# A one-layer encoder on one core: lo parts of weights on VectorE alone, a shorter first pass of the output projection, and a fixed order for the forms of the second norm

## The chip, the cores and the metric

The kernel runs on one core of a Trainium2 chip. A core has TensorE (PE in the views; its weight loads are listed apart as PEld), VectorE (DVE), ScalarE (ACT), GpSimd (POOL) and SyncE (SP), which here starts nearly all the transfers (DMAs) from the chip's memory (HBM). Each engine works through its own queue of instructions in order, and the engines wait for one another by semaphores. The on-chip memory that all of them read is SBUF; PSUM is the small memory into which TensorE writes its sums. The metric is the time of one execution on the device in microseconds (us), and the number to predict is the median of such runs.

## The reference: what is computed

One layer of an encoder over 512 tokens of 1024 channels, in float32. The part before the change's place is told in words here: an RMS norm, one input projection to 7680 columns, a pooling mixer, a differential attention, a two-way gated recurrence, and three sigmoid gates. What the change touches is from the last up-projection to the end:

```python
    gates = jax.nn.sigmoid(gate_pre.reshape(B, S, N_BRANCHES, D_MODEL))
    merged = (gates[:, :, 0] * (y_pool @ w_up_pool[l])
              + gates[:, :, 1] * (y_attn @ w_up_attn[l])
              + gates[:, :, 2] * (y_rec @ w_up_rec[l]))
    x = x + merged @ w_out[l]

    h2 = rms_norm(x, norm2_g[l])
    gu = h2 @ w_ffn_in[l]
    x = x + (jax.nn.silu(gu[..., :FFN_HIDDEN]) * gu[..., FFN_HIDDEN:]) @ w_ffn_out[l]
return rms_norm(x, final_norm_g)
```

The hidden width `FFN_HIDDEN` is 2816.

## The kernel before

**Split numbers.** Every large product is made of three products in a shorter float format (`fp32r`): each operand is split into a hi part, the number rounded to that format, and a lo part, what is left; then hi by hi, lo by hi and hi by lo are added in PSUM. For a weight, `split_w` (L179 to L184) does it: ScalarE copies the raw weight to `whi` (L182) and another engine subtracts `whi` from the raw weight to give `wlo` (L183). Which engine does the subtraction is taken from a cycle, `lo_engine`. It is VectorE alone at first; from the attention's branch through the output projection and the second norm GpSimd and VectorE take turns, beginning with GpSimd; in the first FFN product it is VectorE alone; in the second FFN product the two take turns again.

**Loading and splitting ahead.** `Jobs` holds the list of products in order. A chunk of weights of 1 MB, loaded by SyncE (L161) into one of two raw buffers, holds two parts, and a part is split into one of three pairs of buffers (`wsp`) while earlier products still run. A raw buffer is free for the next load when the lo parts of its chunk are written. The last half of the output projection has a pool of its own for its four parts (`LAST["wp"]`, four pairs), so these parts don't wait for `wsp`.

**Order.** The matmuls keep the order in which the code gives them. On the other engines the framework that builds the program places instructions by a planner of its own (`schedule_with_timeline_sim=True`), which takes what is ready by its own costs, earlier code first. So the order on ScalarE and VectorE is read from the trace and can differ from that of the code; `tc.issue_after(i)` forces an instruction to stand behind `i` when both are on the same engine.

**The up-projection's end.** The last eight products of the attention branch give `merged`, one row tile of 128 channels each: VectorE multiplies the sum by the gate (L582) and adds it to `merged` (L583), ScalarE writes `m_hi` (L586), VectorE writes `m_lo` (L587). These are the k-tiles 0 to 7 of the output projection.

**The output projection.** `w_out` has 1024 columns. Columns 0 to 255 (called Q0 here) and 256 to 511 (Q1) are jobs of `out_quarter_job`, of two parts each: part a holds k-tiles 0 to 3, part b k-tiles 4 to 7. Columns 512 to 1023 are one job, `out_last_job`, of four parts with two k-tiles each (L0 to L3 here). Q0 and Q1 take four blocks of 128 tokens, 8 k-tiles and three terms, so 96 matmuls of 256 columns each. When Q0 starts, the last `m_hi` and `m_lo` aren't there yet; so its first three blocks leave the last k-tile out at first (21 matmuls each), in three open sums, and take it up afterwards. Each block's sum is added to the residual by VectorE (L999, L1008).

**The second norm.** For each of the four blocks: mean square on ScalarE (L405), `rstd` on GpSimd, scaling on VectorE (L411), transposes on TensorE, hi (L424) and lo (L426) of the transposed rows, and a full copy (L428).

**Forms.** The first FFN product multiplies 2 by 2 blocks of weights and rows with seven products in place of eight, so it needs four combinations of row blocks, the forms `n1`, `n2`, `d` and `n4`. `Forms.make` (L324 to L348) has VectorE make the combinations `v` (L341 to L345), ScalarE their hi parts `fhi` (L336) and VectorE their lo parts `flo` (L338). The code's order of the lo parts is `n1`, `n2`, `d`, `n4`. The weights' side needs sums of weights (L260 to L264) with parts `shi` and `slo`.

**The first FFN product.** `ffn_start_job` begins it: two products of the first pair that need no form, and the whole of column tile 0, gate and up, in plain form, whose SiLU and product are `ffn_pair_evac(0)` (L1039, L1040). Then the first pair goes on with `n1` and `n2` (`second`), `d` (`third`) and `n4` (`fourth`). ScalarE copies sums to `u` (L1109) and `g` (L1112); VectorE adds to `g` (L1118) before `n4` may be written to the same bank. The weights of pairs 2 and 3 are split only behind `FF["forms"].last` (`PairPart.split`, L278), which before is the lo part of `n2` on VectorE alone.

**The second FFN product** has 11 steps for each half of the columns, of 24 matmuls of 512 columns; the hidden rows are split by ScalarE (L1056) and VectorE (L1057), and one weight part is split for each step.

Of the kernel before, what the change touches and what calls it, by code (L numbers as in the profile page):

```python
# [11 lines left out]
F32 = mybir.dt.float32  # L12
# [3 lines left out]
ALU = mybir.AluOpType  # L16
PSUM = bass.MemoryType.PSUM

P = 128
# [57 lines left out]
def encoder_kernel(ctx: ExitStack, tc: tile.TileContext, x, norm1_g, w_in, pool_w, pool_scale,  # L77
# [98 lines left out]

    lo_engine = [cycle([nc.vector])]

    def split_w(view, a, b, wpool=None):  # L179
        hi = (wpool or wsp).tile([P, a, b], F32R, name="whi")  # L180
        lo = (wpool or wsp).tile([P, a, b], F32R, name="wlo")
        nc.scalar.copy(out=hi, in_=view)  # L182
        next(lo_engine[0]).tensor_tensor(out=lo, in0=view, in1=hi.bitcast(F32), op=ALU.subtract)  # L183
        return hi, lo  # L184
# [56 lines left out]
    class PairChunk:  # L241
# [14 lines left out]
        def add(self):  # L256
# [7 lines left out]
            nc.vector.tensor_tensor(out=sums[:, 1], in0=sums[:, 3], in1=w12, op=ALU.add)  # L264

    class PairPart:

# [47 lines left out]
    class Forms:  # L315
# [8 lines left out]
        def make(self, pool_, full, v):  # L324
# [8 lines left out]
            order = ("d", "n2", "n1", "n4")  # L333

            def done(i):
                nc.scalar.copy(out=hi[:, i], in_=v[i])  # L336
                setattr(self, order[i], (hi[:, i], lo[:, i]))
                return nc.vector.tensor_tensor(out=lo[:, i], in0=v[i], in1=hi[:, i].bitcast(F32), op=ALU.subtract).ins  # L338

            stt = nc.vector.scalar_tensor_tensor  # L340
# [645 lines left out]
    def out_quarter_job(cs, first):  # L986
        def body(*parts):
            m, x2 = LAST["m"], LAST["x2"]
            pss = {}

            for b in range(3 if first else 0):
                pss[b] = bank("mm")[:, 0:256]
                yield from rows_mm(pss[b], m, slice(b * P, (b + 1) * P), parts, 4, range(KT - 1))
            for b in range(NB):
                ps = pss.get(b)
                if ps is None:
                    ps = bank("mm")[:, 0:256]
                yield from rows_mm(ps, m, slice(b * P, (b + 1) * P), parts, 4, range(KT - 1 if b in pss else 0, KT))
                nc.vector.tensor_tensor(out=x2[:, b, cs], in0=x2[:, b, cs], in1=ps, op=ALU.add)  # L999
        return body  # L1000
# [241 lines left out]

    lo_engine[0] = cycle([nc.gpsimd, nc.vector])
    stM = ExitStack()
# [27 lines left out]
    with ExitStack() as st:  # L1272
        sums = hp2.tile([P, KT, S], F32, name="hid2")
        FF["forms"].make(st.enter_context(pool("forms")), full, sums)
        FF["hid"] = [p.tile([P, 8, S], F32, name=n) for p, n in ((hp2, "hid2"), (hp, "hid"), (hp2, "hid2"))]
        ffn_pair_evac(0, *FF["first"])
        jobs.limit = 4
        lo_engine[0] = cycle([nc.vector])
        pipe.run([jobs.stream(n_ffn - n_out)])
    lo_engine[0] = cycle([nc.gpsimd, nc.vector])  # L1280
    FF["g"] = ctx.enter_context(pool("gf")).tile([P, D], F32, name="gfb")
# [53 lines left out]
```

## Time and profile before

| what | value |
|---|---|
| median of 3 runs | 926.35 us |
| the runs | 932.74, 924.45, 926.35 us |
| the profiled execution | 932.13 us |
| its span, first to last instruction | 930.3 us |
| mean granted TensorE clock | 0.994 |
| TensorE, VectorE, ScalarE, GpSimd busy | 898.0, 578.2, 419.6, 113.0 us |
| lo parts of weights on GpSimd | 19, mean 2399 ns |
| lo parts of weights on VectorE | 127, mean 1168 ns |

Rows of the timeline begin with the start and the duration in us, then the engine, the line, the operation, the tile written and those read, the shapes and the count; in square brackets stands how long the engine was idle before and which instruction ended that. SPq is SyncE's queue. In the rows of windows the busy times of the five engines are followed by the granted TensorE clock (1.00 is full), the share of the DMA engines that was busy, and GB/s. In the view of waits each row gives the total in us, the count and the longest.

### The profile page before, as it was taken

What the parts mean: (1) busy time and instruction counts of PE and PEld (TensorE: products, weight loads), DVE (VectorE), ACT (ScalarE), POOL (GpSimd) and SP (SyncE); (2) the same over time, 40 slices, a digit from 0 to 9 for tenths busy, and PEclk for the clock granted to TensorE, in tenths of its full rate; (3) what the DMA queues carried; (4) which work ended last, traced back from release to release, by engine and by line L of the source; (5) the groups of instructions that cost most, each with busy time, mean ns of one, the idle gap of its engine ahead of it and who ended that gap; (6) DMA issues with size and microseconds to landing.
All of it is one profiled execution on the core that took longest, in us unless ns stands there. A gap on an engine that the chain in (4) does not pass through costs nothing.

```text
span 930.3 us, 13178 instructions
## 1 busy us (share of the span) xinstructions
PE 898.0 (97%) x5341; PEld 790.8 (85%) x5341; DVE 578.2 (62%) x849; ACT 419.6 (45%) x652; POOL 113.0 (12%) x93
## 2 busy tenths in 40 slices
PE   5998999999999999999999989899999999999996
PEld 4887987888898888788888888899999999988885
DVE  5686553754858864634423635998888888635644
ACT  5544423533646673332233324655555555533433
POOL 2143311310000000000022231000000000022222
PEclk9999999999999999999999989999999999999999
DMA  8322031314034115422222450143433433422312
GB/s 248 89 75 68 3 90 34 103 46 153 25 110 132 48 46 170 157 91 91 91 91 91 132 163 1 46 136 94 133 93 99 127 93 104 136 78 91 94 65 91
DMA packets 106313, 89.00 MB, mean 96 GB/s; under 512 B 2687, under 2 KB 93325, under 8 KB 106125
## 3 DMA queue, kind: packets, MB, share of 16 engines
q1 hardware_dynamic: 105532, 86.59, 30.4%
q10 hardware_dynamic: 720, 1.57, 0.4%
q8 instruction: 42, 0.69, 0.3%
q14 instruction: 19, 0.15, 0.0%
HBM read 86.06 MB, written 2.10 MB: 95 GB/s over the span
## 4 chain that ended last, share of the span: by engine, by line
PE 82%; DVE 5%; ACT 1%; issue 1%; POOL 1%; DMA 1%; POOLq 0%; ACTq 0%; DVEq 0%
PE mm L90 56%; PE rc L90 21%; PE tp L90 4%; PE tp L98 1%; DVE wlo L183 1%; DMA raw<-in_w_out_dram 1%; POOL wlo L183 1%; DVE kq L731 1%; ACT whi L182 0%; DVE flo L338 0%; DVE pyr L741 0%; DVE slo L290 0%; DVE sums L260 0%; DVE l L824 0%; DVE pt L746 0%
## 5 line engine op out<-in xcount | busy, mean ns | idle before, releaser
L182 ACT CAST whi<-raw 128x1024 fp32r<-128x1024 f32 (+1 forms) x146 | 143.9, 990 | 208.5 <-PE mm L90 120.3
L183 DVE TENSOR_TENSOR wlo<-raw,whi 128x1024 fp32r<-128x1024 f32 x127 | 148.1, 1168 | 140.4 <-PE mm L90 80.3
L90 PE MATMUL mm<-hT_hi,whi 128*128 128x512 f32 (+1 forms) x440 | 110.0, 387 | 0.4 <-ACT hT_hi L424 0.4
L90 PE MATMUL mm<-hT_hi,wlo 128*128 128x512 f32 (+1 forms) x440 | 108.4, 383 | 0.0
L90 PE MATMUL mm<-hT_lo,whi 128*128 128x512 f32 (+1 forms) x440 | 107.5, 382 | 0.4 <-DVE hT_lo L426 0.4
L183 POOL TENSOR_TENSOR wlo<-raw,whi 128x1024 fp32r<-128x1024 f32 x19 | 45.6, 2399 | 470.1 <-ACT whi L182 351.3
L90 PEld LDWEIGHTS mm<-hT_lo,whi 128*128 128x128 f32 x440 | 79.1, 188 | 15.6 <-DVE hT_lo L426 0.6
L90 PEld LDWEIGHTS mm<-hT_hi,whi 128*128 128x128 f32 x440 | 78.4, 188 | 16.4 <-issue 1.9
L90 PEld LDWEIGHTS mm<-hT_hi,wlo 128*128 128x128 f32 x440 | 78.8, 188 | 15.4 <-issue 1.0
L290 DVE TENSOR_TENSOR slo<-sums,shi 128x1024 fp32r<-128x1024 f32 x42 | 51.4, 1223 | 17.3 <-ACT shi L288 17.3
L288 ACT CAST shi<-sums 128x1024 fp32r<-128x1024 f32 x42 | 44.1, 1050 | 39.9 <-issue 25.6
L1057 DVE TENSOR_TENSOR hlo<-hid,hhi 128x1024 fp32r<-128x1024 f32 x20 | 34.9, 1753 | 25.8 <-ACT hhi L1056 25.8
L734 POOL TENSOR_TENSOR kq<-kq,pyr 128x512 f32<-128x512 f32 x24 | 34.3, 1428 | 45.4 <-ACT kc L700 27.2
L90 PEld LDWEIGHTS rc<-kq,kc 128*128 128x128 f32 x224 | 29.7, 191 | 6.6 <-issue 2.7
L90 PE MATMUL rc<-kq,kc 128*128 128x128 f32 x224 | 32.1, 287 | 2.9 <-DVE kq L731 2.9
L731 DVE TENSOR_TENSOR kq<-kq,pyr 128x256 f32<-128x256 f32 x56 | 26.2, 507 | 14.0 <-PE rc L90 13.9
L700 ACT COPY kc<-kq 128x512 f32<-128x512 f32 x28 | 18.7, 668 | 32.0 <-POOL kq L734 22.8
L858 ACT ACTIVATE s<-s,mx 128x512 f32<-128x512 f32 x32 | 23.0, 720 | 16.1 <-DVE mx L856 16.0
L90 PE MATMUL mm<-flo,shi 128*128 128x256 f32 x168 | 26.7, 281 | 0.9 <-DVE flo L338 0.9
L90 PE MATMUL mm<-fhi,shi 128*128 128x256 f32 x168 | 26.7, 281 | 0.5 <-ACT u L1109 0.5
L90 PE MATMUL mm<-fhi,slo 128*128 128x256 f32 x168 | 26.6, 281 | 0.0
L90 PE MATMUL mm<-y_hi,whi 128*128 128x512 f32 x96 | 26.4, 393 | 0.0
(255 smaller groups left out, 1858.5 us busy)
## 6 DMA issues: line engine op xcount, KB each, us to landing
raw<-in_w_ffn_in_dram SPq DMA_DIRECT2D x44, 512.0 KB, 5.3
raw<-in_w_in_dram SPq DMA_DIRECT2D x18, 1024.0 KB, 5.2
raw<-in_w_in_dram SPq DMA_DIRECT2D x24, 512.0 KB, 4.2
raw<-in_w_ffn_out_dram SPq DMA_DIRECT2D x10, 1024.0 KB, 5.1
raw<-in_w_out_dram SPq DMA_DIRECT2D x4, 1024.0 KB, 5.3
xin<-in_x_dram SPq DMA_DIRECT2D x4, 512.0 KB, 9.0
raw<-in_w_up_rec_dram SPq DMA_DIRECT2D x2, 1024.0 KB, 7.7
x<-in_x_dram SPq DMA_DIRECT2D x1, 2048.0 KB
```

What stands on the lines that cost most here:

```text
L90: i = nc.tensor.matmul(out_, lhsT=lhsT, rhs=rhs, start=start, stop=stop, skip_group_check=chain)
L98: tc.keep_in_program_order(nc.tensor.transpose(out_, in_, idn))
L182: nc.scalar.copy(out=hi, in_=view)
L183: next(lo_engine[0]).tensor_tensor(out=lo, in0=view, in1=hi.bitcast(F32), op=ALU.subtract)
L288: nc.scalar.copy(out=hi, in_=view)
L290: nc.vector.tensor_tensor(out=lo, in0=view, in1=hi.bitcast(F32), op=ALU.subtract)
L700: nc.scalar.copy(out=strided(kc, 0, [[2 * n, S // (2 * n)], [n, 2], [1, n]]), in_=strided(kq, 2 * S, [[2 * n, S // (2 * n)], [S + n, 2], [ ...
L731: nc.vector.tensor_tensor(out=xv, in0=xv, in1=tv, op=ALU.mult)
L734: (nc.gpsimd if n < 128 else nc.vector).tensor_tensor(out=xv, in0=xv, in1=tv, op=ALU.mult)
L858: nc.scalar.activation(out=s, in_=s, func=AF.Exp, scale=-1.0, bias=mx[:, c:c + 1], accum_out=zz[:, i, c:c + 1])
L1057: nc.vector.tensor_tensor(out=lo, in0=view, in1=hi.bitcast(F32), op=ALU.subtract)
```

## The change

It does three things.

First, `lo_engine` is gone and `split_w` always uses VectorE; the 19 subtractions that GpSimd did are VectorE's.

Second, the first three blocks of Q0 leave out the last two k-tiles at first, not the last one: 18 matmuls each, and then six for each in place of three. The number of matmuls is the same.

Third, in `Forms.make` every VectorE instruction is placed behind the one before it, so the order on VectorE is that of the code. `done` returns both its ScalarE and its VectorE instruction. The splits for pairs 2 and 3 now stand behind both of `n2` (before: the VectorE one), and the SiLU and the product of column tile 0 stand behind both of `n4`, on ScalarE and on VectorE; before nothing held them. `issue_after` puts an order on one engine and no wait between engines.

```diff
     def split_w(view, a, b, wpool=None):
...
-        next(lo_engine[0]).tensor_tensor(out=lo, in0=view, in1=hi.bitcast(F32), op=ALU.subtract)
+        nc.vector.tensor_tensor(out=lo, in0=view, in1=hi.bitcast(F32), op=ALU.subtract)
...
+    @contextmanager
+    def behind(after):
+        with ExitStack() as st:
+            for i in after:
+                st.enter_context(tc.issue_after(i))
+            yield
...
         def split(self):
-            with tc.issue_after(FF["forms"].last) if self.chunk.behind else ExitStack():
+            with behind(FF["forms"].last) if self.chunk.behind else ExitStack():
                 self.sums_and_split()
...
+            last = [None]
+            def dve(form, **kw):
+                with tc.issue_after(last[0]) if last[0] else ExitStack():
+                    last[0] = form(**kw).ins
             def done(i):
-                nc.scalar.copy(out=hi[:, i], in_=v[i])
+                on_act = nc.scalar.copy(out=hi[:, i], in_=v[i]).ins
                 setattr(self, order[i], (hi[:, i], lo[:, i]))
-                return nc.vector.tensor_tensor(out=lo[:, i], in0=v[i], in1=hi[:, i].bitcast(F32), op=ALU.subtract).ins
+                dve(tt, out=lo[:, i], in0=v[i], in1=hi[:, i].bitcast(F32), op=ALU.subtract)
+                return on_act, last[0]
...
-            nc.vector.tensor_tensor(out=v[2], in0=f["r11"], in1=f["r12"], op=ALU.subtract)
-            nc.vector.tensor_tensor(out=v[0], in0=f["r22"], in1=f["r12"], op=ALU.subtract)
-            stt(out=v[1], in0=v[0], scalar=-1.0, in1=f["r11"], op0=ALU.mult, op1=ALU.subtract)
+            dve(tt, out=v[2], in0=f["r11"], in1=f["r12"], op=ALU.subtract)
+            dve(tt, out=v[0], in0=f["r22"], in1=f["r12"], op=ALU.subtract)
+            dve(stt, out=v[1], in0=v[0], scalar=-1.0, in1=f["r11"], op0=ALU.mult, op1=ALU.subtract)
             done(2)
-            stt(out=v[3], in0=v[1], scalar=-1.0, in1=f["r21"], op0=ALU.mult, op1=ALU.subtract)
+            dve(stt, out=v[3], in0=v[1], scalar=-1.0, in1=f["r21"], op0=ALU.mult, op1=ALU.subtract)
             self.last = done(1)
             done(0)
-            done(3)
+            self.end = done(3)
...
             for b in range(3 if first else 0):
                 pss[b] = bank("mm")[:, 0:256]
-                yield from rows_mm(pss[b], m, slice(b * P, (b + 1) * P), parts, 4, range(KT - 1))
+                yield from rows_mm(pss[b], m, slice(b * P, (b + 1) * P), parts, 4, range(KT - 2))
...
-                yield from rows_mm(ps, m, slice(b * P, (b + 1) * P), parts, 4, range(KT - 1 if b in pss else 0, KT))
+                yield from rows_mm(ps, m, slice(b * P, (b + 1) * P), parts, 4, range(KT - 2 if b in pss else 0, KT))
...
-        ffn_pair_evac(0, *FF["first"])
+        with behind(FF["forms"].end):
+            ffn_pair_evac(0, *FF["first"])
```

More of the change, by code (lines that the diff above doesn't have):

```diff
@@ L1 @@
-from contextlib import ExitStack
-from itertools import cycle, islice
+from contextlib import ExitStack, contextmanager
+from itertools import islice
 import numpy as np
@@ L175, in split @@
             self.chunk.left -= 1
-    lo_engine = [cycle([nc.vector])]
     def split_w(view, a, b, wpool=None):
@@ L1241, in encoder_kernel @@
         pipe.run([pool_mix(), jobs.stream(n_pool - n_att)])
-    lo_engine[0] = cycle([nc.gpsimd, nc.vector])
     stM = ExitStack()
@@ L1275, in encoder_kernel @@
         FF["hid"] = [p.tile([P, 8, S], F32, name=n) for p, n in ((hp2, "hid2"), (hp, "hid"), (hp2, "hid2"))]
-        ffn_pair_evac(0, *FF["first"])
+        with behind(FF["forms"].end):
+            ffn_pair_evac(0, *FF["first"])
         jobs.limit = 4
-        lo_engine[0] = cycle([nc.vector])
         pipe.run([jobs.stream(n_ffn - n_out)])
-    lo_engine[0] = cycle([nc.gpsimd, nc.vector])
     FF["g"] = ctx.enter_context(pool("gf")).tile([P, D], F32, name="gfb")
```

2 lines of the change are left out of this document (1 added, 1 removed).

## The prediction

> **What bounds the kernel now.** I read the page's first lines, then TensorE's waits, then the timeline around each wait that the change can touch.
>
> ```profile
> span 930.3 us, 13178 instructions
> PE 898.0 (97%) x5341; PEld 790.8 (85%) x5341; DVE 578.2 (62%) x849; ACT 419.6 (45%) x652; POOL 113.0 (12%) x93
> ```
> ```profile
> PE tp L98 <- DVE hT_lo L426: 2.1, 1, 2.1
> PE mm L90 <- ACT whi L182: 1.9, 1, 1.9
> PE mm L90 <- POOL wlo L183: 1.0, 1, 1.0
> PE mm L90 <- DVE flo L338: 0.9, 1, 0.9
> PE mm L90 <- DVE g L1118: 0.9, 1, 0.9
> PE mm L90 <- ACT m_hi L586: 0.6, 1, 0.6
> PE mm L90 <- DVE m_lo L587: 0.6, 1, 0.6
> ```
>
> TensorE is busy for 97% of the span: it is the bound, and only what keeps it waiting can be won. Of the seven waits (total, count, longest) the last six are in reach of this change, 5.9 us together; the first lies near the start and is needed for the clock below. A wait costs more than its row where the clock falls after it, so the output projection (Q0 and Q1) has to be seen in time, by rows of its timeline (many between them are left out) and of its windows:
>
> ```profile
> 517.44 0.69 DVE L583 TENSOR_TENSOR merged<-merged,gate 128x512 f32<-128x512 f32 x1
> 519.82 2.40 POOL L183 TENSOR_TENSOR wlo<-raw,whi 128x1024 fp32r<-128x1024 f32 x1 [8.78 <-ACT whi L182]
> 520.16 2.60 DVE L583 TENSOR_TENSOR merged<-merged,gate 128x512 f32<-128x512 f32 x1
> 524.67 0.87 PE L90 MATMUL mm<-whi,m_hi 128*128 128x256 f32 x6
> 528.53 1.23 DVE L183 TENSOR_TENSOR wlo<-raw,whi 128x1024 fp32r<-128x1024 f32 x1
> 528.79 0.87 PEld L90 LDWEIGHTS mm<-whi,m_hi 128*128 128x128 f32 x7
> 529.35 0.61 ACT L586 CAST m_hi<-merged 128x512 fp32r<-128x512 f32 x1
> 529.52 2.48 POOL L183 TENSOR_TENSOR wlo<-raw,whi 128x1024 fp32r<-128x1024 f32 x1 [7.30 <-ACT whi L182]
> 529.58 0.87 PEld L90 LDWEIGHTS mm<-whi,m_lo 128*128 128x128 f32 x7
> 530.00 2.56 DVE L587 TENSOR_TENSOR m_lo<-merged,m_hi 128x512 fp32r<-128x512 f32 x1 [0.24 <-ACT m_hi L586]
> 532.03 0.37 SPq L161 DMA_DIRECT2D raw<-in_w_out_dram  x1
> 534.20 1.10 DVE L999 TENSOR_TENSOR x<-x,mm 128x256 f32<-128x256 f32 x3 [1.64 <-PE mm L90]
> 537.15 2.94 ACT L182 CAST whi<-raw 128x1024 fp32r<-128x1024 f32 x3 [7.18 <-DMA raw<-in_w_out_dram]
> 537.60 0.63 PE L90 MATMUL mm<-whi,m_hi 128*128 128x256 f32 x4
> 539.22 4.78 POOL L183 TENSOR_TENSOR wlo<-raw,whi 128x1024 fp32r<-128x1024 f32 x2 [7.21 <-ACT whi L182]
> 540.14 0.73 PE L90 MATMUL mm<-whi,m_hi 128*128 128x256 f32 x4 [1.90 <-ACT whi L182]
> 544.05 1.22 PE L90 MATMUL mm<-wlo,m_hi 128*128 128x256 f32 x4 [1.02 <-POOL wlo L183]
> 554.64 0.63 PE L90 MATMUL mm<-whi,m_hi 128*128 128x512 f32 x2
> ```
> ```profile
> 20.00:30.00 10.00, 7.88 (x63) 7.34 (x63) 5.73 (x17) 2.29 (x5) 0.00 (x0) 1.00 0.38 104
> 541.00:542.00 1.00, 1.00 (x8) 1.00 (x8) 0.00 (x0) 0.00 (x0) 1.00 (x2) 0.59 0.00 0
> 548.00:549.00 1.00, 1.00 (x11) 1.00 (x10) 0.15 (x1) 0.00 (x0) 0.00 (x0) 0.99 1.17 292
> ```
>
> Seven matmuls of 256 columns take 529.58 - 528.79 = 0.79 us, so one takes 0.113 and the 96 of Q0 or of Q1 10.85. Q0 runs from 524.67 to 537.60, 2.08 too long: the two waits for k-tile 6 (0.6 and 0.6) and the refilling of TensorE's pipeline after them. Q1 runs from 537.60 to 554.64, 17.04, or 6.19 too long. Of that 1.90 is the wait for the hi part of its part b, 1.02 that for its lo part; the other 3.27 is mostly the clock, which the last two rows (clock: the third figure from the right) show at half from about 541.2 to 548.0, 6.8 us. So 8.27 us stand here against an unhindered TensorE.
>
> Why Q1b comes late can be read too. GpSimd ends L1's lo part at 532.00, which frees a raw buffer; the load of L2 and L3 is issued at 532.03; ScalarE starts at 537.15, on its landing, three hi parts in a row, ending at 540.09; TensorE goes on at 540.14. So the third of the three is Q1b's, and it stands behind L2's and L3's on ScalarE, though the code has it first.
>
> **Part 1: lo parts on VectorE.** Removed: 19 GpSimd subtractions (2.40 each here). Added: 19 on VectorE, 1.23 each. In most places that costs nothing, since TensorE doesn't wait:
>
> ```profile
> 470.00:480.00 10.00, 10.00 (x45) 8.27 (x45) 1.23 (x1) 2.67 (x4) 2.39 (x1) 1.00 0.24 80
> 860.00:870.00 10.00, 10.00 (x46) 8.27 (x45) 8.17 (x11) 5.86 (x10) 1.53 (x2) 1.00 0.32 105
> ```
>
> In the attention's branch VectorE has 8.8 of 10 us free. In the second FFN product the fullest stretch is 860 to 870: 8.17 plus one part, 9.4 of 10. The cover is that parts are split some steps ahead; were it gone there, one late part would cost up to 1.2 us, once. I take 0.
>
> In the output projection it counts. VectorE's subtractions beside GpSimd's are stretched: L583 took 2.60 at 520.16 against 0.69 at 517.44, and L587 2.56. Both end just after GpSimd's. So VectorE gets back 1.9 + 1.9 and takes over two parts of 1.23 there: 1.3 us less load, not more. The Trainium skill, "Perfetto Trace Analysis", section "Optimizing Scalar/DVE Operations", speaks against this move: with VectorE saturated, work offloaded to another engine, GpSimd even, may pay, though it adds that the two share a port, so it might not help. By the first half of that rule 2.5 us of load are added here with none handed back, L1's lo part below ends about 1.9 later and as much of the gain below is gone; the stretched rows side with the second half.
>
> L1's lo part would then follow L0's (ends 529.76). With the last m_lo first (0.7) it ends at 531.9. Before it, and all of VectorE 0.7 earlier (the 1.9 of L583 back, less the 1.23 of Q0b's lo part, which GpSimd did at 519.82), at 530.3. I take 531.1, 0.9 us before GpSimd's end; ends 530.3 and 531.9.
>
> **Part 2: two k-tiles left out.** No instruction more or less. The first pass has 54 matmuls, 6.1 us, and ends at 530.8 without touching k-tiles 6 and 7; the last m_hi ends at 529.96 and the last m_lo, unstretched, at about 530.7 (or 531.9 behind L1's lo part). So both waits go, and Q0 ends at 524.67 + 10.85 = 535.5, 2.1 earlier.
>
> Nearly all of that is eaten at once, for Q1's part b is next, and it hangs on the load, not on TensorE. Load issued at 531.1, the same 5.1 us to ScalarE's start: 536.2. If Q1b's hi part stays third, TensorE goes on at 539.2, second at 538.2; I take 538.8. Q1 has stopped at 535.5 + 0.45 = 536.0, so the wait *grows* from 1.9 to 2.8, but ends 1.3 sooner. Q1b's lo part on VectorE, last of three, ends at 540.9 (537.2 + 3 x 1.23), and TensorE wants it 16 matmuls, 1.8 us, after going on, at 540.6: 0 to 0.3, so about 1 of the 1.02 is gone. The remaining 92 matmuls end at 549.2, plus the clock.
>
> For the clock: 1.9 and 1.02 close together were followed by half speed; the 2.1 us gap in the 20 to 30 row by none (1.00). A single 2.8 us gap may do either; it costs between 0 and the 3.27 above; I take the middle, 1.5. Q1 ends at 550.7: **3.9 us gained** of 8.27. The Trainium skill, "TensorE: Matmul & The Clock Gate", section "Part 1: The HAM clock gate", says that activity is judged in free-running windows of about 3.4 us; the 6.8 us above is two of them, and by that rule a gap with no second wait behind it costs one window, 1.7 us, or nothing, by its phase, which no run need share with another; with 1.7 the gain is 3.7, with 0 it is 5.4.
>
> **Part 3: the forms.**
>
> ```profile
> 589.01 1.28 ACT L1039 ACT_TABLE_LOAD   x1
> 590.80 1.04 ACT L182 CAST whi<-raw 128x1024 fp32r<-128x1024 f32 x1
> 591.75 2.94 ACT L336 CAST fhi<-hid 128x1024 fp32r<-128x1024 f32 x3
> 592.83 1.23 DVE L338 TENSOR_TENSOR flo<-hid,fhi 128x1024 fp32r<-128x1024 f32 x1 [0.92 <-ACT fhi L336]
> 595.10 2.35 DVE L338 TENSOR_TENSOR flo<-hid,fhi 128x1024 fp32r<-128x1024 f32 x2
> 597.51 0.73 PE L90 MATMUL mm<-flo,shi 128*128 128x256 f32 x4 [0.92 <-DVE flo L338]
> 598.73 0.37 ACT L1109 COPY u<-mm 128x256 f32<-128x256 f32 x1 [2.19 <-PE mm L90]
> 600.84 1.22 DVE L338 TENSOR_TENSOR flo<-hid,fhi 128x1024 fp32r<-128x1024 f32 x1
> ```
>
> Before the first `fhi` ScalarE does a table load, the SiLU (together 1.8, 589.01 to 590.80) and a weight part of pair 2 (1.04). VectorE idles 0.92 for the first `fhi`; and TensorE, which wanted the lo part of `n2` at 596.59 (597.51 less 0.92), gets it at the end of the pair that began at 595.10, 597.45: `n2` is the second of that pair, behind `d`. After: the three go behind the forms, so the 0.92 of VectorE goes, and `n2` comes before `d`, another 1.2 earlier. So `n2` is ready at 597.45 - 0.92 - 1.2 = 595.3, and TensorE's 0.92 goes.
>
> The added order holds table load and SiLU until `n4`'s hi part is done: its combination ends before `n2`'s lo part begins, 594.1, plus 1.0 for the hi part and 1.8 is 596.9. Behind them on ScalarE queue the copies to `g` and `u`, and TensorE waits for `u`, now at 598.73, then at 597.8. So 0.9 covers it; if a weight part of pair 2 (1.04) comes between, up to 0.6 is lost. The product L1040 is behind `n4`'s lo part on VectorE, and nothing of TensorE's waits for it here. Late next is the 0.9 for `g` (L1118): VectorE is packed to there, but `n4`'s 1.22 at 600.84 has moved up; so that wait becomes anything from 0 to 0.9, and I take 0.6. Sum: 0.9 + 0.3 = **1.2** gained, ends 0.3 and 1.8.
>
> **The sum** against the profiled execution: 3.9 + 1.2 = 5.1; its time is 930.3 of span and 1.8 around it, 932.1, so 927.0. The median of the runs, 926.35, lies 5.8 below that execution. If its run didn't have the half clock, 2.9 (6.8 less 1.0 of waiting, halved) of my gain isn't there to be had: 2.2, so 924.2; if it had, 921.3. I take the middle, 922.7.
>
> **The rivals.**
>
> *A: the wait for Q1b goes altogether.* ScalarE takes Q1b's hi part first, as soon as Q0 leaves its buffer at about 534.2, before the load of L2 lands. For it: the code's order; Q0 is 2.1 earlier and the load only 0.9. Against it: in the trace the planner put it behind both. Then all of 8.3 goes, with 1.2 for the forms 9.5; by the two readings of the median 916.9 or 919.8, so 918.3.
>
> *B: slower, by VectorE's queue.* L1's lo part lands behind the three L999 additions (534.20 now), which wait for the second pass: the third block's sum is done at 530.8 + 18 x 0.113 = 532.8, its addition by 533.4, then 1.23: 534.6. Load 5.1, three copies 2.94: TensorE goes on at 542.7 after idling 6.7 us; 10.4 and the 3.3 of the clock follow, so Q1 ends at 556.4, 1.8 late. Less 1.2 for the forms it is 0.6 slower than a baseline with the half clock and 3.5 slower than one without: 926.9 or 929.9, so 928.4. It decides from an end of L1's lo part of about 534.1. For it: the planner has put late code ahead of early code here. Against: that part's inputs are ready some 3 us before the last addition's.
>
> *C: part 2 does nothing.* If m_lo of k-tile 6 was never late without the stretched rows, all is part 1's; then the time is that of the forecast, and only the credit differs.
>
> **How the numbers follow.** Forecast (wait shortened at its end but not gone, C included): 0.65; A 0.20; B 0.12; 0.03 for what I don't see. The range takes in A's and B's times: 917 to 929, wide because the three runs span 924.45 to 932.74. One per cent, 9.3 us, is about what a measurement of this kernel can tell from no change. Faster by over 1% is A in its better half and little else: 0.14; slower by over 1%: 0.05; within: 0.81.
>
> **What would show it.** Right: no GpSimd `wlo`; L583 and L587 all near 0.69; no wait for m_hi or m_lo in Q0; the load of L2 issued by 532; a wait for `whi` at Q1's start of 2 to 3 us ending before 539.5; none for `wlo`; none for `flo`. Wrong: that wait absent (A), or past 542 (B), or TensorE waits after 800.

## The result, and the profile after

| what | before | after |
|---|---|---|
| median of 7 runs | 932.74 us | 919.20 us |
| the runs | 924.45 to 933.57 us | 917.68 to 926.52 us |
| the profiled execution | 932.13 us | 917.68 us |
| mean granted TensorE clock in it | 0.994 | 0.997 |

The ratio after to before is 0.990, with a 95% interval of 0.985 to 0.9945. The forecast was 922.7 us with a range of 917 to 929, so the time lies in it, 3.5 us under the likeliest value.

One thing has to be said before any of these numbers is read. The runs of either kernel lie in two groups about 8 us apart, and which group a run falls into goes with a pace of TensorE that is shown further down. Over all the comparisons made here the kernel before was run 71 times: 49 times between 922.75 and 928.58 (middle 925.5) and 22 times between 931.57 and 935.06 (middle 933.6). Of the seven runs in the table four are of the upper group. Of the seven after, six lie between 917.68 and 922.33 (middle 919.0) and one is 926.52. Lower group against lower group, the change is worth 925.5 - 919.0 = 6.5 us; the 13.5 us between the two medians of the table is that and the luck of the groups. The ratio of 0.990 holds some of this luck too: lower group against lower group it is 0.993.

The first two lines of the page after:

```profile
span 915.9 us, 13166 instructions
PE 887.4 (97%) x5341; PEld 781.0 (85%) x5341; DVE 583.4 (64%) x868; ACT 418.9 (46%) x652; POOL 66.8 (7%) x74
```

GpSimd has its 19 subtractions less (93 to 74 instructions, 113.0 to 66.8 us), VectorE 19 more (849 to 868) for only 5.2 us more of busy time, since its own instructions are no longer stretched beside GpSimd's (the additions to `merged`, the `m_lo` and the lo parts of the hidden rows take 16.4 us less together).

To see where the 14.4 us between the two profiled spans (930.3 and 915.9) went, I cut both traces at the first matmul of each stage:

| stage, us | before | after | won |
|---|---|---|---|
| start to Q0 | 524.67 | 524.74 | -0.07 |
| Q0 | 12.93 | 11.31 | 1.62 |
| Q1 | 17.04 | 12.65 | 4.39 |
| L0 to the first matmul of `n4` (second norm and forms lie in it) | 48.41 | 47.40 | 1.01 |
| `n4` to the second FFN product (pairs 1 to 21) | 199.38 | 191.88 | 7.50 |
| second FFN product | 119.45 | 119.47 | -0.02 |

The change's own stages give 1.62 + 4.39 + 1.01 = 7.0 us. The largest row, 7.50, lies where the change does nothing. First the stages it does touch. Rows of the timeline after, in the output projection (the line numbers are those of the kernel after: `whi` L180, `wlo` L181, `merged` L597, `m_lo` L601):

```profile
521.25 0.68 DVE L597 TENSOR_TENSOR merged<-merged,gate 128x512 f32<-128x512 f32 x1
524.74 0.87 PE L90 MATMUL mm<-whi,m_hi 128*128 128x256 f32 x6
527.61 2.36 DVE L181 TENSOR_TENSOR wlo<-raw,whi 128x1024 fp32r<-128x1024 f32 x2 [0.23 <-ACT whi L180]
529.88 0.69 DVE L601 TENSOR_TENSOR m_lo<-merged,m_hi 128x512 fp32r<-128x512 f32 x1
529.99 0.37 SPq L161 DMA_DIRECT2D raw<-in_w_out_dram  x1
535.01 2.94 ACT L180 CAST whi<-raw 128x1024 fp32r<-128x1024 f32 x3 [5.96 <-DMA raw<-in_w_out_dram]
536.05 0.63 PE L90 MATMUL mm<-whi,m_hi 128*128 128x256 f32 x4
538.00 0.74 PE L90 MATMUL mm<-whi,m_hi 128*128 128x256 f32 x4 [1.32 <-ACT whi L180]
548.71 1.54 PE L90 MATMUL mm<-whi,m_hi 128*128 128x512 f32 x6
```
```profile
536.00:543.00 7.00, 5.68 (x48) 5.42 (x48) 4.25 (x5) 2.07 (x4) 0.00 (x0) 1.00 0.42 121
543.00:549.00 6.00, 6.00 (x54) 5.96 (x54) 2.30 (x4) 2.34 (x3) 0.00 (x0) 1.00 1.15 290
```

No stretched L597 or L601 is left (2.60 and 2.56 before). L0's and L1's lo parts run as a pair from 527.61 and end at 529.97, ahead of the last `m_lo`; the load goes out at 529.99 (532.03 before); ScalarE begins 5.0 us later and does three hi parts, and TensorE goes on at 538.00, when the third is done. So Q1b is still the third of the three. Q0 runs without a wait, and the one wait left in Q1 is 1.32 us, with the clock at full speed throughout (the third figure from the right, 1.00 in both rows).

The forms: the addition to `g` in the timeline before, then the timeline after (combinations and `flo` are L346, `fhi` L349, the product of column tile 0 L1054, the addition to `g` L1132):

```profile
602.58 0.42 DVE L1118 TENSOR_TENSOR g<-mm,g 128x256 f32<-128x256 f32 x1
```
```profile
588.16 2.35 DVE L346 TENSOR_TENSOR flo<-hid,fhi 128x1024 fp32r<-128x1024 f32 x2
590.43 1.22 DVE L258 TENSOR_TENSOR sums<-raw 128x1024 f32<-128x1024 f32 x1
591.56 1.82 DVE L181 TENSOR_TENSOR wlo<-raw,whi 128x1024 fp32r<-128x1024 f32 x2
592.02 0.74 PE L90 MATMUL mm<-fhi,shi 128*128 128x256 f32 x4 [0.46 <-ACT u L1123]
593.30 1.22 DVE L346 TENSOR_TENSOR flo<-hid,fhi 128x1024 fp32r<-128x1024 f32 x1
594.44 0.68 DVE L1054 TENSOR_TENSOR hid<-rc,silu 128x512 f32<-128x512 f32 x1
595.04 0.68 DVE L261 TENSOR_TENSOR sums<-sums,raw 128x512 f32<-128x512 f32 x1
595.64 0.41 DVE L1132 TENSOR_TENSOR g<-mm,g 128x256 f32<-128x256 f32 x1
596.11 0.74 PE L90 MATMUL mm<-fhi,whi 128*128 128x256 f32 x4 [1.08 <-DVE g L1132]
```

The lo parts of `n2` and `d` are a pair from 588.16, `n2` first now, and TensorE no longer waits for one. But the wait for `g` is 1.08, not smaller than the 0.89 of before. From the start of that pair to the addition to `g` VectorE does eight instructions without a pause: the lo parts of `n2`, `d` and `n4`, two sums and two lo parts of pair 2, and the product of column tile 0. In before it is the same eight in another order, and both times they take 7.48 us (595.10 to 602.58 before, 588.16 to 595.64 after). The fixed order moves the lo part of `n4` among them; it takes none of them out. What the change moves is their start, from 40.46 us after the first matmul of L0 to 39.45, because VectorE's idle 0.92 before its first `flo` is gone. The addition to `g`, and `n4` behind it, come earlier by that 1.0 and no more.

Now the 7.50 us. The same two windows in both traces, before first; the first two busy times, with their counts, are TensorE's matmuls and its weight loads:

```profile
700.00:710.00 10.00, 10.00 (x88) 10.00 (x87) 8.21 (x10) 5.50 (x11) 0.00 (x0) 1.00 0.39 107
750.00:760.00 10.00, 10.00 (x87) 10.00 (x86) 8.32 (x11) 5.39 (x9) 0.00 (x0) 1.00 0.39 107
```
```profile
700.00:710.00 10.00, 10.00 (x90) 10.00 (x90) 8.71 (x12) 5.34 (x9) 0.00 (x0) 1.00 0.42 118
750.00:760.00 10.00, 10.00 (x91) 10.00 (x89) 8.71 (x11) 5.82 (x10) 0.00 (x0) 1.00 0.42 113
```

TensorE is full, the clock is granted whole, nothing waits, and yet before does 87 to 88 matmuls in 10 us and after 90 to 91. By their starts the matmuls of 256 columns come every 0.118 us before and every 0.113 after, to the end of that product. The stretch holds the 12 matmuls of pair 1's `n4` and 84 for each of 20 pairs, 1692: 199.38 / 1692 = 0.1178 and 191.88 / 1692 = 0.1134, and that is the 7.5 us. In before the products ahead of it ran at 0.113 to 0.114, and 0.118 began with the matmul that ended the wait for `g`. In after it was 0.118 in Q0 and 0.113 after the wait for `whi` that ended at 538.00.

### The profile page after: what moved, and what is told of

Read it like the earlier page. It is cut to its first block, busy times and chain, and to the rows that moved or that the text cites. A ratio compares the mean times of both kernels' runs of the same rounds, so it can differ in the third digit from the quotient of the medians.

```text
span 915.9 us, 13166 instructions
## 1 busy us (share of the span) xinstructions
PE 887.4 (97%) x5341; PEld 781.0 (85%) x5341; DVE 583.4 (64%) x868; ACT 418.9 (46%) x652; POOL 66.8 (7%) x74
## 4 chain that ended last, share of the span: by engine, by line
PE 83%; DVE 6%; DMA 1%; ACT 1%; issue 1%; POOL 1%; POOLq 0%; ACTq 0%; DVEq 0%
PE mm L90 56%; PE rc L90 21%; PE tp L90 4%; DVE wlo L181 2%; PE tp L98 1%; DMA raw<-in_w_out_dram 1%; DVE kq L745 1%; DVE hid L346 0%; DVE flo L346 0%; POOL kq L748 0%; ACT whi L180 0%; DVE pyr L755 0%; DVE sums L258 0%; DVE slo L296 0%; DVE l L838 0%
## 5 line engine op out<-in xcount | busy, mean ns | idle before, releaser
L181 DVE TENSOR_TENSOR wlo<-raw,whi 128x1024 fp32r<-128x1024 f32 (+1 forms) x146 | 170.2, 1169 | 168.5 <-PE mm L90 85.0
L180 ACT CAST whi<-raw 128x1024 fp32r<-128x1024 f32 (+1 forms) x146 | 143.8, 990 | 202.6 <-PE mm L90 116.8
L90 PEld LDWEIGHTS mm<-hT_hi,whi 128*128 128x128 f32 x440 | 78.4, 188 | 16.4 <-issue 1.9
L90 PE MATMUL mm<-y_lo,whi 128*128 128x512 f32 x96 | 26.2, 392 | 0.0
L258 DVE TENSOR_TENSOR sums<-raw 128x1024 f32<-128x1024 f32 x21 | 25.7, 1224 | 0.6
L90 PE MATMUL mm<-y_hi,wlo 128*128 128x512 f32 x96 | 25.9, 390 | 0.0
L90 PE MATMUL mm<-flo,shi 128*128 128x256 f32 x168 | 25.9, 276 | 0.0
```

Of the source, the lines that this page charges most:

```text
L90: i = nc.tensor.matmul(out_, lhsT=lhsT, rhs=rhs, start=start, stop=stop, skip_group_check=chain)
L181: nc.vector.tensor_tensor(out=lo, in0=view, in1=hi.bitcast(F32), op=ALU.subtract)
L258: nc.vector.tensor_tensor(out=strided(sums, 0, [[2 * half, 2], [1, half]]), in0=strided(self.raw, 0, [[3 * half, 2], [1, half]]), in1=stri ...
```

## The experiments

The kernel before ran beside each group of experiments (e1 to e4, e5 to e8, e9), on the same chip as the group; the three groups ran on three chips. "Lower group" is the middle of those runs that are not of the slower pace, with their count; for the kernel before it is 925.5.

| run | median, us | ratio to before, 95% interval | lower group | Q0 + Q1 | L0 to `n4` | `n4` to second FFN |
|---|---|---|---|---|---|---|
| after | 919.20 | 0.990 (0.985 to 0.9945) | 919.0 (6 of 7) | 23.96 | 47.40 | 191.88 |
| e1_lo_only | 920.67 | 0.994 (0.991 to 0.997) | 920.6 (10 of 12) | 23.98 | 48.40 | 191.88 |
| e2_kt_only | 919.90 | 0.994 (0.991 to 0.997) | 919.8 (10 of 12) | 23.75 | 48.41 | 191.88 |
| e3_forms_only | 923.96 | 0.999 (0.9965 to 1.002) | 923.7 (9 of 12) | 29.61 | 47.40 | 191.88 |
| e4_q1b_first | 917.95 | 0.990 (0.987 to 0.9935) | 917.9 (9 of 11) | 22.61 | 47.41 | 191.88 |
| e5_round_trip | 959.67 | 1.035 (1.031 to 1.039) | all 6 in one group | 28.15 | 48.42 | 226.37 |
| e6_splits_behind_n4 | 918.35 | 0.990 (0.987 to 0.994) | 918.4 (7 of 7) | 24.14 | 47.50 | 191.76 |
| e7_both_orders | 918.07 | 0.9915 (0.988 to 0.995) | 917.3 (10 of 12) | 22.61 | 47.44 | 191.85 |
| e8_before_again | 934.26 (one run) | | upper | 29.88 | 48.41 | 199.38 |
| e9_dve_behind_n4 | 916.56 | 0.988 (0.983 to 0.993) | 916.2 (5 of 6) | 22.61 | 46.81 | 191.98 |

### e1_lo_only: part 1 alone

```diff
-        next(lo_engine[0]).tensor_tensor(out=lo, in0=view, in1=hi.bitcast(F32), op=ALU.subtract)
+        nc.vector.tensor_tensor(out=lo, in0=view, in1=hi.bitcast(F32), op=ALU.subtract)
```

> Before with part 1 alone (lo parts on VectorE; one k-tile left out, forms as before). My theory now: this part carries the whole gain of the output projection. In the changed kernel m_hi and m_lo of k-tile 6 are done at 524.3 and 525.0, before even the old first pass would want them (525.4 and 526.2), so both waits of Q0 go without part 2, the load of L2 is issued near 530 and columns 512 and up start at 548 to 549 (before 554.6, changed kernel 548.7). Rival: part 2 is needed for half of it, then the waits for m_hi and m_lo stay at 0.5 us or more each and that start is at 550 or later. The flo wait of 0.9 stays under both. Time: 6 us less than before where both have the same pace of 256-column matmuls in the first FFN product (0.113 or 0.118 us each), about 0.993 as a ratio.

Its timeline (lines as in the kernel before):

```profile
528.00 2.36 DVE L183 TENSOR_TENSOR wlo<-raw,whi 128x1024 fp32r<-128x1024 f32 x2 [0.20 <-ACT whi L182]
530.28 0.68 DVE L587 TENSOR_TENSOR m_lo<-merged,m_hi 128x512 fp32r<-128x512 f32 x1
538.44 0.74 PE L90 MATMUL mm<-whi,m_hi 128*128 128x256 f32 x4 [1.36 <-ACT whi L182]
```

The picture of the kernel after, down to the wait (1.36 against 1.32), and Q0 + Q1 is 23.98 against 23.96. Both waits of Q0 for k-tile 6 are gone although the first pass still touches k-tile 6: without the stretched L583 and L587 that tile isn't late. So with part 1 in place part 2 adds nothing.

### e2_kt_only: part 2 alone

```diff
-                yield from rows_mm(pss[b], m, slice(b * P, (b + 1) * P), parts, 4, range(KT - 1))
+                yield from rows_mm(pss[b], m, slice(b * P, (b + 1) * P), parts, 4, range(KT - 2))
...
-                yield from rows_mm(ps, m, slice(b * P, (b + 1) * P), parts, 4, range(KT - 1 if b in pss else 0, KT))
+                yield from rows_mm(ps, m, slice(b * P, (b + 1) * P), parts, 4, range(KT - 2 if b in pss else 0, KT))
```

> Before with part 2 alone (two k-tiles left out; GpSimd and VectorE take turns as before). My theory: Q0 loses its two waits and ends 1 to 2 us sooner, but Q1's part b hangs on GpSimd's lo part of L1 and the load behind it, so its wait grows from 1.9 to 3 or 4 us and still ends at 540.1, and columns 512 and up start within 1 us of 554.6: no gain. Rival: part 2 is worth the 1.2 us of the two waits or more, start at 553.4 or earlier. Ratio 1.000 under the first, 0.998 under the second.

The theory failed. Rows of its timeline:

```profile
530.41 2.55 DVE L587 TENSOR_TENSOR m_lo<-merged,m_hi 128x512 fp32r<-128x512 f32 x1 [0.24 <-ACT m_hi L586]
533.02 0.39 PE L90 MATMUL mm<-whi,m_lo 128*128 128x256 f32 x1 [0.99 <-DVE m_lo L587]
536.57 3.16 ACT L182 CAST whi<-raw 128x1024 fp32r<-128x1024 f32 x3 [6.19 <-PE mm L90]
```

GpSimd still stretches the last `m_lo` (2.55), and TensorE waits 0.99 for it. But look at what ended ScalarE's idle time before the three hi parts: in before and after it is the landing of the load (`DMA raw`), here it is a matmul. ScalarE takes Q1b's hi part first, as soon as Q0 gives its buffer back, and the wait for `whi` in Q1 is gone altogether, though the load of L2 and L3 goes out as late as before (532.45). That is the prediction's rival A, by another part than I had thought of. The edit changes only the order of the matmuls, so that flipped the planner's order on ScalarE; but in the kernel after the matmuls stand in this order too, and Q1b's hi part is third again. By what rule the planner chooses isn't in the traces. Parts 1 and 2 thus bring the same 6 us each alone, by different routes, and together no more than one of them.

### e3_forms_only: part 3 alone

The diff is that of `Forms.make`, `behind`, `split` and `ffn_pair_evac` in the change.

> Before with part 3 alone (forms in a fixed order). My theory: it is worth 1.0 us up to the n4 product of the first pair and no more; the pace of the 256-column matmuls in the first FFN product (0.1133 us in the changed kernel's trace, 0.1178 before, 7.5 us in all) is a state that a wait of TensorE leaves behind by chance and not an effect of any part, so this kernel shows one of the two, and its runs fall into two groups 8 us apart as those of before do (924 to 926 and 933). Rival: the order of the forms is what removed the slow pace; then all runs lie in the fast group less 1, near 924, and the trace shows 0.1133. Ratio 0.999 or, by the rival, about 0.992.

The stretch from L0 to `n4` is 47.40, the very number of the kernel after, so part 3 is worth 1.0 us in the profile and is independent of the others; the ratio of the runs can't tell that from no change. The pace in its profile is 0.113, but 3 of its 12 runs (931.30, 932.46, 932.87) are of the upper group: a fixed order of the forms doesn't cure the slow pace. Q0 + Q1 still has all four waits (0.63, 0.60, 1.65 and 1.77). The granted clock falls once here; its windows:

```profile
541.00:545.00 4.00, 2.23 (x18) 2.03 (x18) 0.00 (x0) 0.00 (x0) 3.64 (x2) 1.00 0.33 95
545.00:549.00 4.00, 4.00 (x23) 4.00 (x22) 1.65 (x2) 1.04 (x1) 0.00 (x0) 0.57 1.13 303
549.00:553.00 4.00, 4.00 (x37) 4.00 (x36) 0.84 (x2) 0.00 (x0) 0.00 (x0) 1.00 1.16 290
```

### e4_q1b_first: ScalarE's order written out

The kernel after, with the hi parts of L2 and L3 behind Q1b's on ScalarE:

```diff
-            self.hi, self.lo = split_w(self.view(self.chunk.raw), self.a, self.b, self.wpool)
+            with tc.issue_after(self.behind.hi_copy) if self.behind else ExitStack():
+                self.hi, self.lo = split_w(self.view(self.chunk.raw), self.a, self.b, self.wpool)
+            self.hi_copy = hi_copy[0]
...
+    for p in out_parts[2:]:
+        p.behind = last_quarter[1]
```

> The changed kernel, with the hi parts of L2 and L3 placed behind Q1b's on ScalarE. My theory: the 1.3 us wait left at Q1's start is only this order; Q1b's hi part then starts when Q0 leaves its buffer, near 535, the wait is gone and columns 512 and up start at 547.3 (changed kernel 548.7). Rival: the buffer comes free too late or the later hi parts of L2 and L3 delay something, then that start stays at 548.5 or moves past it. Ratio to before: 1.4 us below the changed kernel's.

```profile
531.39 0.37 SPq L161 DMA_DIRECT2D raw<-in_w_out_dram  x1
536.49 2.95 ACT L185 CAST whi<-raw 128x1024 fp32r<-128x1024 f32 x3 [6.06 <-PE mm L90]
```

Columns 512 and up start at 548.95, where the rival put them; but this execution entered Q0 at 526.34, 1.6 us later than that of the kernel after, since its clock stood at half for 3.41 us near 24. Counted from there Q0 and Q1 take 22.61 us against 23.96, as the theory has it. Again ScalarE's idle time ends by a matmul and not by the load. TensorE has no wait left in the output projection, and Q0 and Q1 take 11.31 us each: 96 matmuls at the slow pace of 0.118, and nothing else. The lower group moves by 919.0 - 917.9 = 1.1, the stages by 1.35. So the wait that the change leaves is the order of three copies on ScalarE, as the prediction read it.

### e5_round_trip and e8_before_again: whose is the pace?

e5 is the kernel before with one addition, for the pairs 2 to 21:

```diff
+            if j > 1:
+                ps = bank("tp")[:, 0:P]
+                transpose(ps, ident, ident)
+                back = FF["t"].tile([P, P], F32, name="back", bufs=1)
+                nc.scalar.copy(out=back, in_=ps)
+                transpose(bank("tp")[:, 0:P], back, ident)
             c["x"], c["zy"] = bank("mm")[:, 0:256], bank("rc")
```

> The kernel before, with one thing added: at the start of each of the pairs 2 to 21 of the first FFN product TensorE writes a 128x128 transpose, ScalarE copies it to SBUF, and TensorE transposes that copy, so TensorE has to stop 20 times for a trip to ScalarE and back, some 1 to 2 us each. It leaves nothing out. In the profile of the kernel before, the 256-column matmuls of pairs 1 to 21 came every 0.118 us after a wait at 603; in the profile after, every 0.113 after a wait at 538, to the end of that product; that is 7.5 us between the two. Theory (the pace is drawn anew each time TensorE stops): among the 20 stretches between the stops of this profile both paces are found, and the runs lie in one group, their two clusters 8 us apart gone, with less than 4 us between most of them. Rival (the pace belongs to the execution or to the chip's state, not to the stop): all 20 stretches have one pace, and the runs keep two clusters about 8 us apart. The time itself is 20 to 40 us above the kernel before, by either.

> The kernel before, unchanged, for one more profile. Theory (the 8 us between the two clusters of its runs are the pace of the 256-column matmuls): if this execution takes 930 to 935 us, the stretch from n4 to the second FFN product is about 199 us long and its matmuls come every 0.118 us; if it takes 923 to 927, about 192 and 0.113. Rival (the clusters come from something else, the clock or the transfers): time and pace don't go together.

Three of the twenty stops of e5, and then groups of four matmuls inside the first and the second stretch between stops, from its timeline:

```profile
606.59 0.33 PE L98 MATMUL tp<-ident,back 128*128 128x128 f32 x1 [1.96 <-ACT back L1100]
617.58 0.33 PE L98 MATMUL tp<-ident,back 128*128 128x128 f32 x1 [1.01 <-ACT back L1100]
628.92 0.33 PE L98 MATMUL tp<-ident,back 128*128 128x128 f32 x1 [1.00 <-ACT back L1100]
```
```profile
609.95 0.62 PE L90 MATMUL mm<-flo,shi 128*128 128x256 f32 x4
610.41 0.62 PE L90 MATMUL mm<-fhi,slo 128*128 128x256 f32 x4
...
621.05 0.64 PE L90 MATMUL mm<-flo,shi 128*128 128x256 f32 x4
621.52 0.64 PE L90 MATMUL mm<-fhi,slo 128*128 128x256 f32 x4
```

Four matmuls take 0.46 us in the first stretch (609.95 to 610.41) and 0.47 in the second (621.05 to 621.52). Over the 19 whole stretches, 8 have a median step of 0.113 and a length of 10.99 to 11.00 us, and 11 have 0.118 and 11.33 to 11.34; none changes on its way. The two follow one another in a pattern: fast, slow, fast, slow, slow, and the same again, to the end. And the six runs lie within 3.3 us (958.96 to 962.22), in one group. So the pace isn't a property of the execution or of the chip that day: in this execution it is set anew at a stop of TensorE and kept to the next. That the pattern is so regular speaks for the phase at which TensorE is set going again; the phase itself isn't in the trace.

e8 closes the other half: the unchanged kernel took 934.26 us this time, and its window has the count of the slow pace.

```profile
700.00:710.00 10.00, 10.00 (x87) 10.00 (x87) 8.31 (x11) 5.39 (x9) 0.00 (x0) 1.00 0.39 107
```

All eleven profiles fit: the two of upper-group runs (932.13 and 934.26) have 199.38 from `n4` to the second FFN product, the eight of lower-group runs 191.76 to 191.98, and e5 has both paces. The granted clock doesn't part the groups: its median is 0.993 over 46 lower-group runs of the kernel before and 0.994 over 17 upper-group ones. No upper-group run of the kernel after or of its variants was profiled.

### e6, e7 and e9: what `n4` waits for

e6 places the splits of pairs 2 and 3 behind `n4` on both engines, e7 does that and e4 together, and e9 does e4 and holds them behind `n4` on VectorE alone (the edits for `n4` of e6 and e9):

```diff
-            with behind(FF["forms"].last) if self.chunk.behind else ExitStack():
+            with behind(FF["forms"].end) if self.chunk.behind else ExitStack():
```
```diff
+            with behind((FF["forms"].last[0], FF["forms"].end[1])) if self.chunk.behind else ExitStack():
```

> The kernel after, with the splits of pairs 2 and 3 placed behind both of n4's instructions, not behind n2's. Theory (the wait of 1.08 us for g that is left is VectorE's order: a sum of 1.22 and two lo parts of 0.91 of pair 2 stand between d's lo part and n4's, and a sum of 0.68 before the addition to g): n4's lo part moves from 593.30 to about 590.5 and the wait for g to between 0 and 0.5, the stretch from the start of L0 to the first matmul of n4 from 47.40 to 46.4 to 46.9; nothing of pair 2 comes late, since its first weights are wanted only some 6 us later; 0.5 to 1.0 us faster than the kernel after. Rival (the load of VectorE as a whole sets the addition to g, not the order): the wait stays at about 1, or comes back as a wait for pair 2's lo parts or sums, and the stretch stays at 47.4.

> The kernel after with both orders written out: the hi parts of L2 and L3 behind that of Q1b on ScalarE, and the splits of pairs 2 and 3 behind both of n4's instructions. If the two are as separate as they look: Q0 and Q1 together 22.6 us as with the first alone (after: 23.96), the stretch from L0 to n4 46.4 to 46.9, so 1.9 to 2.4 us under the kernel after and 8 to 10 under the kernel before, at like pace of the matmuls. If the earlier L0 takes the cover from the forms (rival), the stretch from L0 to n4 stays at 47.4 and the sum of the two is 1.4.

The timeline of e6:

```profile
590.14 3.49 DVE L346 TENSOR_TENSOR flo<-hid,fhi 128x1024 fp32r<-128x1024 f32 x3
593.12 1.55 ACT L180 CAST whi<-raw 128x1024 fp32r<-128x1024 f32 x2
594.58 0.37 ACT L1126 COPY g<-rc 128x256 f32<-128x256 f32 x1
594.84 0.39 ACT L1123 COPY u<-mm 128x256 f32<-128x256 f32 x1
595.28 0.74 PE L90 MATMUL mm<-fhi,shi 128*128 128x256 f32 x4 [1.73 <-ACT u L1123]
597.62 0.42 DVE L1132 TENSOR_TENSOR g<-mm,g 128x256 f32<-128x256 f32 x1
598.21 0.62 PE L90 MATMUL mm<-fhi,whi 128*128 128x256 f32 x4
```

The three lo parts are one run now, with the lo part of `n4` ahead of all of pair 2's work on VectorE. Yet the addition to `g` comes no sooner: it begins 7.48 us after the first of the three, as in the kernel after, and 46.91 us after the first matmul of L0 (after: 46.93). The same eight instructions stand ahead of it. So the theory failed and the rival held: the work that VectorE has to do before the addition sets its time, not the place of `n4` in it. The matmul at 598.21 has no wait for `g` only because TensorE comes there later: the two hi parts of pair 2, held back on ScalarE too, now stand ahead of the copies to `g` and `u`, and the wait for `u` has grown from 0.46 to 1.73. One wait was traded for another, 47.50 against 47.40. In e7 the same happens (47.44), so its second order is worth nothing; its gain is e4's.

> The kernel after with the hi parts of L2 and L3 behind that of Q1b on ScalarE (as e4_q1b_first), and the splits of pairs 2 and 3 behind n4's lo part on VectorE, but on ScalarE behind n2's hi part only, as in the kernel after. In e6_splits_behind_n4 the wait for g went, but two hi parts of pair 2 (1.55 us) came between the SiLU and the copy to u on ScalarE, and the wait for u grew from 0.46 to 1.73. Theory (the two waits are set by the two engines' orders one by one): the wait for u stays at about 0.5, that for g is 0 to 0.3, the stretch from the start of L0 to the first matmul of n4 is 46.3 to 46.7 (e4_q1b_first: 47.41), and the kernel is some 0.7 to 1.1 us faster than that one at like pace of the matmuls, 1.0 to 1.4 and 0.7 to 1.1 faster than the kernel after, so a profile near a span of 914. Rival (VectorE has more work ahead of the addition to g than fits): the wait for g, or a new one for pair 2's lo parts, holds the stretch at about 47.4.

```profile
590.20 3.49 DVE L351 TENSOR_TENSOR flo<-hid,fhi 128x1024 fp32r<-128x1024 f32 x3
594.05 0.74 PE L90 MATMUL mm<-fhi,shi 128*128 128x256 f32 x4 [0.46 <-ACT u L1131]
596.47 0.69 DVE L1062 TENSOR_TENSOR hid<-rc,silu 128x512 f32<-128x512 f32 x1
597.07 0.42 DVE L1140 TENSOR_TENSOR g<-mm,g 128x256 f32<-128x256 f32 x1
597.40 0.69 DVE L266 TENSOR_TENSOR sums<-sums,raw 128x512 f32<-128x512 f32 x1
597.55 0.74 PE L90 MATMUL mm<-fhi,whi 128*128 128x256 f32 x4 [0.40 <-DVE g L1140]
```

With ScalarE's order left alone the wait for `u` is back at 0.46, and that for `g` falls from 1.08 to 0.40. One of the eight instructions, the second sum of pair 2 (0.69 at 597.40), now stands behind the addition, so 6.87 us lie between 590.20 and 597.07 in place of 7.48. Two lo parts and a sum of pair 2 and the product into `hid` (L1062) still stand ahead, so the wait stays above the 0 to 0.3 expected. The stretch is 46.81, 0.6 less than in e4 where 0.7 to 1.1 was expected. At 916.56 us it has the lowest median of the versions tried, 0.983 to 0.993 of the kernel before, an interval that overlaps those of e4, e6 and e7. Of its gain over the kernel after (lower groups 919.0 and 916.2, of 6 and 5 runs) the stages give 1.35 to ScalarE's order and 0.6 to VectorE's; the rest they don't show.

## Why the prediction was right, and where it was not

**The way of the gain was right.** The forecast was a wait for Q1b that ends earlier but doesn't go. That is what the trace shows: no `wlo` on GpSimd, L583 and L587 back at 0.69, no wait in Q0, the load out before 532, Q1b third of three, TensorE going on before 539.5, no wait for `wlo` and none for `flo`. One sign didn't come: the wait itself is 1.32 us and not 2 to 3. The Trainium skill's page "Perfetto Trace Analysis", section "Optimizing Scalar/DVE Operations", has two halves on such a move; e1 sides with the one on the shared port: 19 subtractions went to VectorE, and the work around them ended earlier (L587 took 0.68 there against 2.56 before).

**The output projection's term was too small: 3.9 predicted, 6.0 measured.** The clock (1.5 taken of 0 to 3.27) cost nothing: it stayed at 1.00 in the profiled execution. That is in part luck, since it may fall after the same wait in one execution and not in another (last section). TensorE went on 0.8 earlier than taken; the matmuls behind that took 10.7 us, 0.3 more. The 0.8 comes from L1's lo part, which, taken at 531.1 with ends of 530.3 and 531.9, ended at 529.97: the planner put it as a pair with L0's ahead of the last `m_lo`. The load, ScalarE's start (5.0 us later, 5.1 taken) and TensorE's (538.00) followed, 1.2 earlier by this, less the 0.4 by which 538.8 had been taken ahead of the time for Q1b as third. And the wait didn't grow to 2.8 but fell to 1.32: it ended 0.8 earlier, and it began 0.7 later, mostly because Q0 ended at 536.05 and not at 535.5. Q0 ran at 0.118 a matmul, not at the 0.113 that I had read off one group. That cost no time: it only shortened the wait.

**Rival C held.** I had costed part 2 as if both it and part 1 were needed for Q0's waits; e1 shows part 1 enough. What I didn't see is that part 2 alone gives rival A's order on ScalarE (e2). Rival A was priced right in its mechanism (e2, e4), and at 0.20 it was not the way of the change as a whole. Rival B didn't occur: L1's lo part ended 4.1 us ahead of the time from which it decides.

**The forms' term was near: 1.2 predicted, 1.0 measured.** The wait for `flo` went as said, with VectorE's 0.92 of idle time, which is nearly all of the gain; the wait for `u` stayed at 0.46. The step that failed is the wait for `g`, put at 0.6 because `n4`'s lo part had moved up. It was 1.08. VectorE is full up to the addition, and where `n4`'s lo part stands in its work changes nothing: the same eight instructions take 7.48 us in the kernels before and after, and in e6, where `n4`'s lo part is ahead of all of pair 2's. The wait shortened, to 0.40, only where one of the eight went behind the addition (e9).

**The step from the profiled execution to the median was wrong in its reason.** I put the 5.8 us between that execution and the median down to half a clock in the output projection that other runs might not have. e8 has the same total in Q0 and Q1 (29.88), with 3.4 us of half clock in place of 6.8, and is as slow as the profiled execution; the 7.5 us are in the first FFN product, by the pace. I looked at the stretch after `n4` for waits only, found none, and didn't read its step. The faster runs don't lack the half clock either: the median of their clocks, 0.993, is no higher than the profiled execution's 0.994 (outside the profiles only a run's mean clock is known, not where it fell). So in most of them the gain that I took off for the missing half clock, up to 2.9, was there to be had: from 925.5 the stages' 7.0 leads to 918.5, and 919.0 was measured. Not in all: e5, the kernel before up to that point, passed Q0 and Q1 without a half clock in 28.15 us, 1.8 less than the profiled execution. And the lower-group runs spread with the clock, from 922.75 at 0.998 to 928.58 at 0.990.

**What stays open.** Whether the change makes the slow pace rarer: 22 of 71 runs before had it, 1 of 7 after, and of e1, e2, e4, e6, e7 and e9 together 9 of 60. A stop can set the pace, and the kernels differ in their stops, so it may; it was not tried apart.

## What to carry to other kernels

Two edits that each remove a wait can be worth no more together than one alone, so look whether the second still has anything to remove, and try each alone: a planner may reach the same end by another order. On an engine that is full, a new order within a group brings nothing forward that still has the same work ahead of it: add up all that stands between the group's start and the instruction that is waited for, put some of it behind that instruction, and do so only on the engine where it does harm. And where an engine is full and waits for nothing, compare the step of its instructions between two profiles before explaining a difference by waits.

## What the runs showed of the hardware

**Two paces of a full TensorE.** Matmuls of 256 columns with their weights loaded each time came every 0.113 or every 0.118 us at a granted clock of 1.00, for up to 199 us on end. The pace changed at breaks in TensorE's stream, of 0.1 us at 534.7 in before and of 0.07 at 533.7 in e1; once it changed without one, from 0.118 to 0.113 at 598.21 in e6, at the first matmul of `n4`. What picks the pace is not shown. Matmuls of 512 columns came every 0.227 in all profiles. The Trainium skill, "TensorE: Matmul & The Clock Gate", section "Part 1: The HAM clock gate", gives for back-to-back bf16 matmuls on a warm array the columns over 2.4 GHz and about 2.5 ns, which would be 0.109 (an estimate by that page); it has no second pace, and the runs here show two.

**The clock falls in whole windows, and not by the length of the wait.** In the output projection half clock lasted 6.83 us after waits of 1.90 and 1.02 us (before), 3.41 after 1.65 and 1.77 (e3) and 3.41 after 2.08 and 1.80 (e8), and didn't come after 1.62 and 1.81 (e5) nor after 1.32 (after). A wait near 22 us, 2.02 to 2.53 us long in all eleven profiles, went with 3.41 us of half clock, beginning between 23.5 and 25.9, in five (e4, e5, e6, e8, e9) and with none in six; the unchanged kernel is among both, with none after 2.12 in before and a fall after 2.17 in e8. In every profile the clock changed only at whole multiples of 3.413 us after it was first granted in full (in before at 155, 157 and 268 of them). The same section of the Trainium skill says that activity is judged in free-running windows of about 3.4 us; these runs agree.
